# Two copies out of PSUM, a later place for the down projection's weight sums, and one PSUM tile moved from one pool to another

## The chip, the cores and the metric

The kernel runs on one core of a Trainium2 chip. The metric is the device time of one execution in microseconds (us); lower is better. The kernel before takes 2284.2 us (median of three runs, 2281.11 to 2285.95). The profile was taken from one more execution, whose own time is 2281.2 us; its span, from the first to the last recorded instruction, is 2279.5 us.

## The reference

The program computes a decoder trunk of two residual layers on 1024 tokens of width 1024. Each layer has a token mixer (layer 0: a gated MLP and dilated attention; layer 1: gated linear attention) and, behind it, a gated feed-forward network with a causal convolution. The change touches the feed-forward part and the end of the mixer's output projection before it:

```
x = x + mix
h = rms_norm(x, norm_ffn_g[layer])
g = causal_dwconv(h @ w_gate, conv_w, conv_b)        # width 3
x = x + (silu(g) * (h @ w_up)) @ w_down              # D_FF = 2816
```

All values are float32.

## The kernel before

**Products.** TensorE multiplies numbers of a reduced float32 format (F32R). To keep float32's accuracy every operand is split into a high part (ScalarE, "ACT", rounds it: the cast in line 92) and a low part (VectorE, "DVE", subtracts: line 93). A product then takes three passes: high by high, high by low, low by high. One 512x128 by 512x512 product is 12 matmuls of 128x512.

**Seven products for eight.** The feed-forward matrices are multiplied in 2x2 blocks by a scheme with seven block products (of the Strassen-Winograd kind): sums of blocks take the place of the eighth product. `ffn_up` walks over pairs of feature tiles, f = 0, 2, ..., 20, and has two streams for each, "g" (gate) and "u" (up). A stream takes products in the order 1, 5, 6, 2, 7, 4, 3, and product 1 of the next stream is opened before 4 and 3 of the current one. Its left operands are weight blocks, or the sums S1 to S4 of weight blocks (line 211, on GpSimd, "POOL", but for the first pair on DVE). Its right operands lie ready in SBUF: the normalised tokens in `hq`, and sums of them in the three tiles `T3`.

**Banks.** Products 1, 6, 7 and 4 add up in one PSUM bank, called B. Products 5 and 3 add up in bank C, product 2 has bank A. Between them the values are taken out: after 1 ACT copies B to `s1` (line 244), after 2 DVE adds `s1` and A to the block C11 (246), after 6 ACT copies B to C12 (248), after 7 ACT copies B to C22 (250) and DVE adds bank C, which then holds product 5 alone, to it (251); after 4 ACT copies B to C21 (253), after 3 DVE adds C, now products 5 and 3, to C12 (255). Matmuls of product 3 write to bank C, so they come behind the reading in line 251. The name `pgB6` is bank B of the gate stream of f = 6, and `wg6p7` is the left operand of its product 7. Banks B and C come from a pool `m1`, bank A and the transposes of the norm from a pool `pt`.

**After the streams.** Behind a pair's "g" stream follow the convolution (`conv`, lines 262 to 269: ACT scales, DVE adds two shifted terms, ACT applies silu) and `down_weights`, which loads two feature tiles of w_down (`rd`), forms four sums of their blocks on DVE (D, lines 280 to 283) and stores them to DRAM (`wsd`), for the down projection. Behind the "u" stream the two results are multiplied (line 324), and `down_acts` forms and stores sums of them (`actd`). The sums S and D and the temporaries of the norm share one ring of four SBUF tiles (tag "S"), and all loaded weights one ring of four (tag "raw").

**Ramp.** Before the streams `out_second` makes the second half of the output projection token tile by token tile (products `po`), normalises each tile (line 129 squares, 133 scales), transposes it on TensorE (line 143, two PSUM tiles `pt` for each token tile) and brings it into the operands (lines 420 to 440). The `pt` tiles are freed by DVE (line 420, tiles 0 to 3) or ACT (line 428, tiles 4 to 7).

**Order.** The code's order gives priorities; a scheduler at compile time fixes one order of instructions for each engine, and waits between engines are semaphores. An engine runs its list strictly in order.

Of the kernel before, what the change touches and what calls it, by code (L numbers as in the profile page):

```python
# [54 lines left out]
def trunk(ctx: ExitStack, tc: tile.TileContext, a, out):  # L55
    nc = tc.nc
    V, A, G, T, Q = nc.vector, nc.scalar, nc.gpsimd, nc.tensor, nc.sync
# [37 lines left out]
    def load_raw(src, name, cols=D):  # L95
        raw = rawp.tile([P, D], F32, tag="raw", name=name)[:, :cols]
        Q.dma_start(raw, src)
        return raw

    def parts_of(src, name, pool=None, **tag):  # L100

        w = (pool or wp).tile([P, 2, 512], F32R, **(tag or {"tag": "w"}), name=name)
        parts = [w[:, i, : src.shape[-1]] for i in range(2)]
        split(parts, src)
        return parts
# [86 lines left out]
    def ffn_up(l, T3, ps, pool, norm_end):  # L192
        cw = pool.tile([P, NF, 3], F32, name=f"cw{l}")
        Q.dma_start(cw, a["conv_w"][l])
        cb = pool.tile([P, NF], F32, name=f"cb{l}")
        Q.dma_start(cb, a["conv_b"][l])
        right = {1: hq[0][0], 2: hq[1][0], 3: hq[1][1], 4: hq[0][1], 5: T3[0], 6: T3[1], 7: T3[2]}

        def stream(kind, f):

            src = a["w_gate" if kind == "g" else "w_up"]
            ra, rb = (load_raw(src[l, f + i], f"r{kind}{f + i}") for i in range(2))
            A11, A12, A21, A22 = ra[:, :512], ra[:, 512:], rb[:, :512], rb[:, 512:]
            out = pool.tile([P, 2, S], F32, tag=kind, bufs=1, name=f"{kind}{f}")
            (C11, C12), (C21, C22) = ([out[:, i, c] for _, c in HALVES] for i in range(2))
            s1 = pool.tile([P, 512], F32, tag="s1", bufs=2, name=f"s1{kind}{f}")
            sums, bank, made = {}, {}, {}

            def summed(name, x, y, op):
                sums[name] = pool.tile([P, 512], F32, tag="S", bufs=4, name=f"{name}{kind}{f}")  # L210
                (G if f else V).tensor_tensor(sums[name], x, y, op=op)  # L211
                return sums[name]

            def left(p):
                if p == 5:
                    return summed("S1", A21, A22, ALU.add)
                if p == 6:
                    return summed("S2", sums["S1"], A11, ALU.subtract)
                if p == 7:
                    return summed("S3", A11, A21, ALU.subtract)  # L220
                if p == 3:
                    return summed("S4", A12, sums["S2"], ALU.subtract)
                return {1: A11, 2: A12, 4: A22}[p]

            def prep(p):
                made[p] = parts_of(left(p), f"w{kind}{f}p{p}")

            def step(p):
                if p not in made:
                    prep(p)  # L230
                L = made[p]

                b = {2: "A", 5: "C", 3: "C"}.get(p, "B")
                more = b in bank
                if not more:
                    bank[b] = ps.tile([P, 512], F32, tag="pt" if b == "A" else "m1", name=f"p{kind}{b}{f}")
                o = bank[b]
                for j in range(4):
                    for ii, jj in PASSES:
                        T.matmul(o, L[ii][:, j * P : j * P + P], right[p][:, jj, j, :], skip_group_check=more,  # L240
                                 start=(not more and j == 0 and (ii, jj) == PASSES[0]),
                                 stop=(j == 3 and (ii, jj) == PASSES[-1]))
                if p == 1:
                    A.copy(s1, o)
                elif p == 2:
                    V.tensor_add(C11, s1, o)
                elif p == 6:
                    A.copy(C12, o)
                elif p == 7:
                    A.copy(C22, o)  # L250
                    V.tensor_add(C22, C22, bank["C"])
                elif p == 4:
                    A.copy(C21, o)  # L253
                elif p == 3:
                    V.tensor_add(C12, C12, o)  # L255

            return step, out, prep

        def conv(f, g2):
            ts = []  # L260
            for i in range(2):
                g = g2[:, i, :]
                t = pool.tile([P, S], F32, tag="t", bufs=4, name=f"t{f + i}")
                w = lambda j: cw[:, f + i, j : j + 1]
                A.activation(t, g, AF.Identity, bias=cb[:, f + i : f + i + 1], scale=w(2))  # L265
                V.scalar_tensor_tensor(t[:, 1:], g[:, : S - 1], w(1), t[:, 1:], op0=ALU.mult, op1=ALU.add)  # L266
                V.scalar_tensor_tensor(t[:, 2:], g[:, : S - 2], w(0), t[:, 2:], op0=ALU.mult, op1=ALU.add)
                A.activation(t, t, AF.Silu)
                ts.append(t)
            return ts  # L270

        def put(dst, f, p, src):
            Q.dma_start(dst[l][p][f // 4][:, f // 2 % 2, :], src)

        def down_weights(f):

            ra, rb = (load_raw(a["w_down"][l, f + i], f"rd{f + i}") for i in range(2))
            A11, A21, A12, A22 = ra[:, :512], ra[:, 512:], rb[:, :512], rb[:, 512:]
            S = {p: pool.tile([P, 512], F32, tag="S", bufs=4, name=f"D{p}{f}") for p in (5, 6, 7, 3)}
            V.tensor_add(S[5], A21, A22)  # L280
            V.tensor_sub(S[6], S[5], A11)
            V.tensor_sub(S[7], A11, A21)
            V.tensor_sub(S[3], A12, S[6])
            for p in S:
                put(wsd, f, p, S[p])

        def down_acts(f, t0, t1):

            (B11, B12), (B21, B22) = ([t[:, c] for _, c in HALVES] for t in (t0, t1))
            x, y = (pool.tile([P, 2, 512], F32, tag="t", bufs=4, name=f"{n}{f}") for n in "xy")  # L290
            right = {1: B11, 2: B21, 3: B22, 5: x[:, 0], 6: x[:, 1], 7: y[:, 0], 4: y[:, 1]}
            V.tensor_sub(right[5], B12, B11)
            V.tensor_sub(right[6], B22, right[5])
            V.tensor_sub(right[7], B22, B12)
            V.tensor_sub(right[4], B21, right[6])
            for p in right:
                put(actd, f, p, right[p])

        todo = [(kind, f) for f in range(0, NF, 2) for kind in "gu"]
        cur, nxt = stream(*todo[0]), stream(*todo[1])  # L300
        for step, _, _ in (cur, nxt):
            step(1)
            step(2)
            if step is cur[0]:
                for prep, p in ((nxt[2], 1), (nxt[2], 2), (cur[2], 5)):
                    prep(p)
                norm_end()
        for i, (kind, f) in enumerate(todo):
            step, out, _ = cur
            early = (1, 2) if i < 2 else (1,)  # L310
            for p in (5, 6, 2, 7):
                if p not in early:
                    step(p)
            if 0 < i < len(todo) - 1:
                nxt = stream(*todo[i + 1])
                nxt[0](1)
            step(4)
            step(3)
            if kind == "g":
                ts = conv(f, out)  # L320
                down_weights(f)
            else:
                for j in range(2):
                    V.tensor_mul(ts[j], ts[j], out[:, j, :])  # L324
                down_acts(f, *ts)
            cur = nxt


# [572 lines left out]
    def banks(st, **bufs):  # L901
        return Tagged({t: st.enter_context(tc.tile_pool(name="psf_" + t, bufs=b, space=PSUM, reuse_waits="tile"))
                       for t, b in bufs.items()})
# [4 lines left out]
    ps = banks(pss, mm=3, pt=2)  # L908
    for l in range(2):
# [22 lines left out]
        with tc.tile_pool(name=f"T{l}", bufs=1, reuse_waits="tile") as tp:  # L932
            T3 = [tp.tile([P, 2, 4, 512], F32R, name=f"T{l}{i}") for i in range(3)]
            pss.close()
            with ExitStack() as st, tc.tile_pool(name=f"fu{l}", bufs=1, reuse_waits="tile") as fp:
                ps = banks(st, m1=6, pt=2)
                norm_end = out_second(l, w_out, x_in, T3, ps, fp)
                ffn_up(l, T3, ps, fp, norm_end)
        ps = banks(pss, mm=3, pt=2)
# [99 lines left out]
```

## Time and profile before

| what | before |
|---|---|
| median of three runs | 2284.2 us |
| profiled execution, its time / its span | 2281.2 us / 2279.5 us |
| PE (matmul) busy | 2193.6 us, 96% |
| DVE busy | 1443.9 us, 63% |
| ACT busy | 968.8 us, 43% |
| POOL busy | 453.3 us, 20% |
| share of PE in the chain of waits that ended last | 73% |

PE is busy for nearly the whole span, so the time is PE's work plus the moments in which it waits or runs at a lower granted clock. The feed-forward streams run from about 525 to 972 us in layer 0 and from about 1620 to 2065 us in layer 1. Times of single instructions are given in microseconds from the span's start.

### The profile page before, as it was taken

To read this page: it belongs to the slowest core of one execution; us is meant where nothing else is said; L and a number is where in the kernel's file an instruction comes from. 1 tells how busy PE (TensorE), PEld (TensorE's weight loads), DVE (VectorE), ACT (ScalarE), POOL (GpSimd) and SP (SyncE) were. 2 spreads that over 40 slices of the span, in tenths; PEclk is the share of its full clock that TensorE was granted. 3 is DMA by queue.
4 is the path that set the end of the run, shared out by engine and by line. 5 is a ranking of instruction groups with operands and counts; after the bars stand their busy time and mean duration, and the time that the engine had idled before them with its cause. 6 is when DMAs were issued, how large, how long until landed. Compare 5 with 4: busy or idle time off the path is not lost.

```text
span 2279.5 us, 29790 instructions
## 1 busy us (share of the span) xinstructions
PE 2193.6 (96%) x10800; PEld 1855.7 (81%) x10800; DVE 1443.9 (63%) x2430; ACT 968.8 (43%) x1786; POOL 453.3 (20%) x487
## 2 busy tenths in 40 slices
PE   7989988997999999999999999999899999999999
PEld 6989977886888888778889888878678887887887
DVE  7566655448777877755574444244787878776554
ACT  5444445235444343434454333223554444444443
POOL 4333220001242424100010111000133333230000
PEclk9999999998999999999999999999999999999999
DMA  4122212343354545475562111355254454457555
GB/s 145 47 73 78 60 50 61 124 145 106 130 171 141 178 137 168 157 282 185 202 224 75 54 54 51 121 180 184 71 171 162 148 170 149 141 178 263 199 190 203
DMA packets 139540, 320.74 MB, mean 141 GB/s; under 512 B 15824, under 2 KB 40400, under 8 KB 139392
## 3 DMA queue, kind: packets, MB, share of 16 engines
q1 hardware_dynamic: 139392, 318.83, 42.0%
q8 instruction: 85, 1.39, 0.2%
q14 instruction: 63, 0.52, 0.1%
HBM read 223.81 MB, written 94.96 MB: 140 GB/s over the span
## 4 chain that ended last, share of the span: by engine, by line
PE 73%; DVE 11%; DMA 6%; issue 5%; ACT 3%; POOL 2%; SPq 0%; DVEq 0%; POOLq 0%; ACTq 0%
PE puB L240 8%; PE pgB L240 7%; PE po L171 6%; PE pv L171 5%; PE pdB L345 5%; PE pdC L345 5%; PE pgC L240 5%; PE pj L171 4%; PE pdO L345 4%; PE pr L171 4%; PE puC L240 3%; PE puA L240 2%; PE pdQ L345 2%; PE pdP L345 2%; PE pk L183 2%
## 5 line engine op out<-in xcount | busy, mean ns | idle before, releaser
L93 DVE TENSOR_TENSOR da<-ar,da 128x512 fp32r<-128x512 f32 x154 | 106.3, 690 | 156.6 <-ACT da L92 156.3
L92 ACT CAST da<-ar 128x512 fp32r<-128x512 f32 x154 | 95.9, 623 | 214.8 <-PE pdC L345 94.7
L171 PE MATMUL po<-wo,hq 128*128 128x512 f32 x768 | 183.9, 394 | 2.2 <-ACT hq L395 1.3
L171 PEld LDWEIGHTS po<-wo,hq 128*128 128x128 f32 x768 | 141.9, 188 | 31.4 <-ACT hq L395 2.3
L171 PE MATMUL pj<-wq,hq 128*128 128x384 f32 x768 | 157.5, 353 | 1.5 <-ACT hq L92 1.5
L171 PE MATMUL pv<-wv,hq 128*128 128x256 f32 (+2 forms) x960 | 154.9, 314 | 0.7 <-ACT gv L507 0.6
L171 PEld LDWEIGHTS pv<-wv,hq 128*128 128x128 f32 x960 | 133.8, 191 | 9.3 <-ACT gv L507 1.0
L171 PEld LDWEIGHTS pj<-wq,hq 128*128 128x128 f32 x768 | 137.3, 197 | 2.2 <-ACT hq L92 1.9
L345 PE MATMUL pdB<-dw,da 128*128 128x512 f32 x528 | 136.4, 391 | 1.7 <-DVE u L255 1.6
L345 PE MATMUL pdC<-dw,da 128*128 128x512 f32 x528 | 135.8, 390 | 0.0
L345 PEld LDWEIGHTS pdB<-dw,da 128*128 128x128 f32 x528 | 98.5, 188 | 23.7 <-DVE u L255 2.4
L211 POOL TENSOR_TENSOR S1u<-ru 128x512 f32<-128x512 f32 x20 | 41.2, 2059 | 384.0 <-DMA wsd<-D 251.0
L93 DVE TENSOR_TENSOR dw<-wr,dw 128x512 fp32r<-128x512 f32 x154 | 105.8, 687 | 16.2 <-ACT dw L92 15.9
L345 PEld LDWEIGHTS pdC<-dw,da 128*128 128x128 f32 x528 | 99.1, 188 | 20.5
L121 POOL TENSOR_SCALAR rn<-ssq 128x1 f32<-128x1 f32 x32 | 8.5, 267 | 475.2 <-ACT h L129 257.3
L345 PE MATMUL pdO<-dw,da 128*128 128x512 f32 x396 | 102.2, 389 | 0.1
L92 ACT CAST dw<-wr 128x512 fp32r<-128x512 f32 x154 | 95.0, 617 | 13.6 <-DMA wr<-in_w_dn 7.7
L171 PE MATMUL pr<-wr,hq 128*128 128x512 f32 x384 | 97.9, 404 | 0.0
L345 PEld LDWEIGHTS pdO<-dw,da 128*128 128x128 f32 x396 | 74.3, 188 | 15.9 <-DVE dw L93 0.6
L171 PEld LDWEIGHTS pr<-wr,hq 128*128 128x128 f32 x384 | 71.2, 188 | 14.5
L324 DVE TENSOR_TENSOR t<-t,u 128x1024 f32<-128x1024 f32 x44 | 75.6, 1717 | 5.4 <-ACT u L253 4.8
L266 DVE SCALAR_TENSOR_TENSOR t<-g,cw,t 128x1023 f32<-128x1023 f32 x44 | 56.5, 1324 | 6.9 <-ACT t L265 6.8
(905 smaller groups left out, 5106.4 us busy)
## 6 DMA issues: line engine op xcount, KB each, us to landing
ar<-actd SPq DMA_DIRECT2D x70, 512.0 KB, 3.6
rg<-in_w_gate SPq DMA_DIRECT2D x44, 512.0 KB, 5.1
ru<-in_w_up SPq DMA_DIRECT2D x44, 512.0 KB, 3.6
rd<-in_w_down SPq DMA_DIRECT2D x44, 512.0 KB, 3.6
wsd<-D SPq DMA_DIRECT2D x88, 256.0 KB, 2.3
wr<-wsd SPq DMA_DIRECT2D x40, 512.0 KB, 4.3
actd<-t SPq DMA_DIRECT2D x66, 256.0 KB, 5.5
wr<-in_w_dn SPq DMA_DIRECT2D x30, 512.0 KB, 4.7
```

Of the source, the lines that this page charges most:

```text
L92: (hi or A.copy)(dst[0], src)
L93: (lo or V.tensor_sub)(dst[1], src, f32(dst[0]))
L121: G.tensor_scalar(r, ssq, 1.0 / n, EPS, op0=ALU.mult, op1=ALU.add)
L171: T.matmul(o, L[i], R[jj][:, sl], start=(k == 0 and (ii, jj) == PASSES[0]), stop=(k == nk - 1 and (ii, jj) == PASSES[-1]))
L183: T.matmul(ps[h], L[i], hq[k % 2][h][:, jj, k // 2, :], start=(k == 0 and (ii, jj) == PASSES[0]), stop=(k == KD - 1 and (ii, jj) == PASSES ...
L211: (G if f else V).tensor_tensor(sums[name], x, y, op=op)
L240: T.matmul(o, L[ii][:, j * P : j * P + P], right[p][:, jj, j, :], skip_group_check=more, start=(not more and j == 0 and (ii, jj) == PASSES ...
L266: V.scalar_tensor_tensor(t[:, 1:], g[:, : S - 1], w(1), t[:, 1:], op0=ALU.mult, op1=ALU.add)
L324: V.tensor_mul(ts[j], ts[j], out[:, j, :])
L345: T.matmul(o, L[ii][:, t * P : t * P + P], R[jj], skip_group_check=more, start=start and not more and (ii, jj) == PASSES[0], stop=stop and ...
```

## The change

Three edits. Product 5 has an evacuation of its own: right behind it ACT copies bank C to C22. Behind product 7 ACT copies bank B to `s1` (free again by then) and DVE adds `s1` to C22, both from SBUF. The call of `down_weights` moves from the end of the pair's "g" stream to the end of its "u" stream, behind `down_acts`. And in the two pools of PSUM that `out_second` and `ffn_up` use, `m1` has 5 tiles in place of 6, `pt` has 3 in place of 2.

```
                 elif p == 6:
                     A.copy(C12, o)
+                elif p == 5:
+                    A.copy(C22, o)
                 elif p == 7:
-                    A.copy(C22, o)
-                    V.tensor_add(C22, C22, bank["C"])
+                    A.copy(s1, o)
+                    V.tensor_add(C22, C22, s1)
...
             if kind == "g":
                 ts = conv(f, out)
-                down_weights(f)
             else:
                 for j in range(2):
                     V.tensor_mul(ts[j], ts[j], out[:, j, :])
                 down_acts(f, *ts)
+                down_weights(f)
...
-                ps = banks(st, m1=6, pt=2)
+                ps = banks(st, m1=5, pt=3)
```

Lines behind the edit move by two: the copies and adds of the list above are lines 250 to 257 in the changed kernel. The scheduler makes another order of all that lies in the ramps and the streams; the rest of the program stands as before. Three places follow.

TensorE in the middle of the streams (f = 6, layer 0), the kernel before:

```order
L240 MATMUL pgB6_6560<-T02_5153,wg6p7_6678 128x512 x12
L240 MATMUL puB6_6704<-hq00_83,wu6p1_6701 128x512 x12
L240 MATMUL puC6_6783<-T00_5151,wu6p5_6780 128x512 x10
L240 MATMUL pgB6_6560<-hq01_84,wg6p4_6718 128x512 x12
L240 MATMUL pgC6_6628<-hq11_86,wg6p3_6736 128x512 x12
L240 MATMUL puC6_6783<-T00_5151,wu6p5_6780 128x512 x2
L240 MATMUL puB6_6704<-T01_5152,wu6p6_6798 128x512 x12
```

The same place in the changed kernel:

```order
L240 MATMUL pgB6_6550<-T02_5153,wg6p7_6685 128x512 x12
L240 MATMUL puB6_6711<-hq00_83,wu6p1_6708 128x512 x2
L240 MATMUL pgC6_6634<-hq11_86,wg6p3_6743 128x512 x12
L240 MATMUL puC6_6774<-T00_5151,wu6p5_6771 128x512 x8
L240 MATMUL pgB6_6550<-hq01_84,wg6p4_6725 128x512 x12
L240 MATMUL puC6_6774<-T00_5151,wu6p5_6771 128x512 x4
L240 MATMUL puB6_6711<-T01_5152,wu6p6_6790 128x512 x12
```

Product 3 (`pgC6`, operand `wg6p3`) stands two matmuls behind product 7 now and ahead of product 4; before, it stood 34 matmuls behind product 7, after product 4.

ACT at the same place, from the end of pair 6's gate stream on, in the kernel before:

```order
L250 COPY g6_6555<-pgB6_6560 128x512
L92 CAST wg8p1_6856<-rg8_6850 128x512
L244 COPY s1u6_6700<-puB6_6704 128x512
L92 CAST wu6p4_6873<-ru7_6697 128x512
L253 COPY g6_6555<-pgB6_6560 128x512
L92 CAST wu6p3_6891<-S4u6_6889 128x512
L92 CAST wg8p5_6924<-S1g8_6922 128x512
L92 CAST wg8p6_6942<-S2g8_6940 128x512
L265 ACTIVATE t6_6752<-g6_6555,cb0_5665,cw0_5663 128x1024
L265 ACTIVATE t7_6757<-g6_6555,cb0_5665,cw0_5663 128x1024
L248 COPY u6_6699<-puB6_6704 128x512
```

And in the changed kernel:

```order
L252 COPY s1g6_6546<-pgB6_6550 128x512
L92 CAST wg8p1_6848<-rg8_6842 128x512
L244 COPY s1u6_6707<-puB6_6711 128x512
L92 CAST wu6p4_6865<-ru7_6704 128x512
L92 CAST wu6p3_6883<-S4u6_6881 128x512
L267 ACTIVATE t6_6759<-g6_6545,cb0_5665,cw0_5663 128x1024
L255 COPY g6_6545<-pgB6_6550 128x512
L267 ACTIVATE t7_6764<-g6_6545,cb0_5665,cw0_5663 128x1024
L250 COPY u6_6706<-puC6_6774 128x512
L270 ACTIVATE t6_6759<-t6_6759 128x1024
L92 CAST wg8p5_6932<-S1g8_6930 128x512
L248 COPY u6_6706<-puB6_6711 128x512
```

The copy of product 5 (line 250) is new, and the copy of bank B to C12 of the u stream (line 248) stands right behind the cast of `S1g8`, a sum that now takes its SBUF tile from the stored sums D of pair 6.

DVE where the streams begin (layer 0, f = 0), the kernel before:

```order
L93 TENSOR_TENSOR wg0p3_5856<-S4g0_5854,wg0p3_5856 128x512
L280 TENSOR_TENSOR D50_5886<-rd0_5882,rd1_5884 128x512
L281 TENSOR_TENSOR D60_5887<-D50_5886,rd0_5882 128x512
L282 TENSOR_TENSOR D70_5888<-rd0_5882 128x512
L283 TENSOR_TENSOR D30_5889<-rd1_5884,D60_5887 128x512
L211 TENSOR_TENSOR S1u0_5898<-ru1_5675 128x512
```

And in the changed kernel:

```order
L211 TENSOR_TENSOR S4g0_5855<-rg0_5667,S2g0_5802 128x512
L211 TENSOR_TENSOR S1u0_5883<-ru1_5675 128x512
L93 TENSOR_TENSOR wg0p6_5804<-S2g0_5802,wg0p6_5804 128x512
L93 TENSOR_TENSOR wg0p7_5822<-S3g0_5820,wg0p7_5822 128x512
L93 TENSOR_TENSOR wg0p4_5839<-rg1_5669,wg0p4_5839 128x512
L93 TENSOR_TENSOR wg0p3_5857<-S4g0_5855,wg0p3_5857 128x512
L211 TENSOR_TENSOR S2u0_5902<-S1u0_5883,ru0_5673 128x512
```

The first sum of the up stream, `S1u0`, stands ahead of the first sum D of w_down now (that one comes ten rows behind the last row shown); before, it stood behind all four.

## Rows read from the trace of the kernel before

**Rows 1.** The page, busy us and share of the span by engine.

```profile
PE 2193.6 (96%) x10800; PEld 1855.7 (81%) x10800; DVE 1443.9 (63%) x2430; ACT 968.8 (43%) x1786; POOL 453.3 (20%) x487
```

**Rows 2.** Windows over both feed-forward parts: ramp (two), streams, end; each layer.

```profile
core 0: us, PE busy (x) PEld busy (x) DVE busy (x) ACT busy (x) POOL busy (x), PEclk, DMA share, GB/s
518.00:546.00 28.00, 22.95 (x105) 17.92 (x104) 25.52 (x43) 20.27 (x45) 3.39 (x4) 0.88 0.13 43
546.00:570.00 24.00, 17.27 (x60) 12.66 (x59) 17.70 (x29) 8.58 (x16) 3.72 (x3) 0.86 0.58 175
570.00:957.00 387.00, 383.14 (x1686) 315.95 (x1685) 299.12 (x339) 166.83 (x261) 131.15 (x78) 1.00 0.48 157
957.00:975.00 18.00, 15.64 (x67) 11.98 (x66) 14.40 (x18) 9.25 (x13) 0.00 (x0) 1.00 0.40 117
1612.00:1640.00 28.00, 23.00 (x102) 18.20 (x102) 24.68 (x41) 19.29 (x44) 3.39 (x4) 0.88 0.08 29
1640.00:1658.00 18.00, 14.18 (x52) 10.26 (x52) 13.73 (x23) 5.94 (x11) 0.00 (x0) 0.91 0.42 134
1658.00:2050.00 392.00, 385.86 (x1697) 317.93 (x1696) 305.41 (x346) 167.94 (x266) 135.67 (x80) 1.00 0.49 159
2050.00:2068.00 18.00, 15.68 (x66) 11.97 (x65) 14.59 (x18) 9.25 (x13) 0.00 (x0) 1.00 0.38 120
```

**Rows 3.** PE's waits by releaser, 505 to 990 and 1590 to 2085: total, times, longest.

```profile
PE pgC L240 <- DVE g L251: 3.9, 4, 1.0
PE puC L240 <- ACT wu0p L92: 3.6, 1, 3.6
...
PE pgC L240 <- DVE g L251: 6.1, 5, 2.1
```

**Rows 4.** Chain that ended last, layer 0, 640 to 720: start, us, what.

```profile
660.96 3.61 DMA rd<-in_w_down
...
665.41 2.03 DMA wsd<-D
...
667.66 2.07 POOL S1u L211
...
679.59 1.70 DVE y L294
...
681.95 3.02 PE pgC L240 x12
...
685.42 2.72 PE puB L240 x12
```

**Rows 5.** Timeline of ACT, layer 0: start, us, line, instruction, idle before.

```profile
579.23 1.28 ACT L268 ACT_TABLE_LOAD   x1
...
659.02 0.59 ACT L250 COPY u<-puB 128x512 f32<-128x512 f32 x1 [1.66 <-PE puB L240]
...
669.75 0.62 ACT L92 CAST wu6p<-S1u 128x512 fp32r<-128x512 f32 x1 [2.44 <-POOL S1u L211]
...
686.09 2.38 ACT L265 ACTIVATE t<-g,cb,cw 128x1024 f32<-128x1024 f32 x2
```

**Rows 6.** Line 251 on DVE: ns min/median/max, first and last start.

```profile
L251 DVE TENSOR_TENSOR g<-g,pgC x22: 672/674/681, 562.5 to 2042.2; 128x512 f32<-128x512 f32 x22
```

**Rows 7.** Chain that ended last, ramp of layer 0.

```profile
561.31 1.22 PE puC L240 x2
562.53 5.10 PE pgB L240 x12
```

**Rows 8.** Timeline of DVE, ramp of layer 0.

```profile
506.53 0.75 DVE L133 TENSOR_SCALAR xt<-xt,rn 128x1024 f32<-128x1024 f32 x1 [2.55 <-DMA xd<-xt]
...
516.80 0.75 DVE L133 TENSOR_SCALAR xt<-xt,rn 128x1024 f32<-128x1024 f32 x1 [2.35 <-ACT n L428]
```

**Rows 9.** Timeline of PE, end of the streams of layer 0.

```profile
965.83 3.02 PE L240 MATMUL puB<-hq,wu20p 128*128 128x512 f32 x12 [1.31 <-ACT u L250]
...
972.35 1.66 PE L345 MATMUL pdB<-dw,da 128*128 128x512 f32 x6 [0.78 <-DVE u L255]
```

More of the change, by code (lines that the diff above doesn't have):

```diff
@@ L248, in step @@
                     A.copy(C12, o)
+                elif p == 5:
+                    A.copy(C22, o)
                 elif p == 7:
-                    A.copy(C22, o)
-                    V.tensor_add(C22, C22, bank["C"])
+                    A.copy(s1, o)
+                    V.tensor_add(C22, C22, s1)
                 elif p == 4:
@@ L320, in ffn_up @@
                 ts = conv(f, out)
-                down_weights(f)
             else:
@@ L325, in ffn_up @@
                 down_acts(f, *ts)
+                down_weights(f)
             cur = nxt
@@ L935, in trunk @@
             with ExitStack() as st, tc.tile_pool(name=f"fu{l}", bufs=1, reuse_waits="tile") as fp:
-                ps = banks(st, m1=6, pt=2)
+                ps = banks(st, m1=5, pt=3)
                 norm_end = out_second(l, w_out, x_in, T3, ps, fp)
```

## Prediction

> **What bounds the kernel now.** I read the page's busy line first: PE is busy for 96% of the span, DVE for 63%, ACT for 43%, POOL for 20% [rows 1]. PE works 2193.6 of 2279.5 us, so no edit that leaves its matmuls alone can give more than some 86 us. The number of matmuls stays. What can be won is PE's idle time in the stretches whose order changes, and matmuls that ran there at a lower clock. The windows give the ceiling [rows 2]: window less PE busy is 5.05 and 6.73 us in the two parts of layer 0's ramp, 3.86 in its streams, 2.36 at their end; in layer 1 it is 5.00, 3.82, 6.14 and 2.32. That is 20.6 us in ramps, 10.0 in streams, 4.7 at the ends. The clock is full in streams and at the ends (PEclk 1.00) and 0.86 to 0.91 in the ramps.
>
> The waits then say what the idle time is. In the streams there is one kind: product 3's first matmul waits for DVE's line 251, 3.9 us in four waits in layer 0 and 6.1 in five in layer 1 [rows 3], which is all of the 3.86 and 6.14. The chain through such a place shows why DVE is late [rows 4]: a load `rd` of w_down (3.61 us) starts at 660.96, a store `wsd` of a sum D (2.03) at 665.41, POOL's sum S1u, whose SBUF tile that store frees, at 667.66, and later a 1.70 us subtraction on DVE, behind which line 251 comes; `pgC` follows at 681.95. Line 251 itself is short (0.67 us) [rows 6]; it stands in DVE's in-order list behind work that waited for weights.
>
> **The change part by part: streams.** The bank C of a "g" stream is now freed by ACT's copy right behind product 5; by the order product 3 follows 48 matmuls later (10.9 us), and nothing of DVE stands between. The 10.0 us go unless something else is late next. What is late next I count backward and forward in PE's slots. A product is 12 matmuls of 2.72 us together [rows 4], 0.227 each. I take the end of the g stream's product 3 as zero. Product 7 ends two matmuls and product 3 earlier, at −3.2. ACT then has a copy (0.59 [rows 5]), a cast, a copy and a cast (0.62 each cast), to −0.8; DVE takes the low half of that operand (about 0.7, as any of its 128x512 work in rows 6), to −0.1. That frees the weight tile into which `rd` is loaded. Its load 3.61: at 3.5. First sum D 0.7: 4.2. Store 2.03 [rows 4]: 6.3. POOL's S1 of the next gate stream 2.07: 8.4. ACT's cast of it: 9.0. Behind this cast stands the copy of B to C12 in the u stream (line 248), 0.59: 9.6. Product 7 of u, which writes to that bank, has its slot at 13.4: between zero and it stand u's 5, 6 and 2, g's 4 and eleven matmuls of the next gate's 1, 59 x 0.227. So the new wait of ACT has 3.8 us of cover. Product 5 of the next gate stream is due 25 matmuls later, 19.0, and has its operand at about 10.7: 8 us of cover. The copy after product 7 must be done before product 4, 5 us later. Five tiles of `m1` are enough: a bank B lives some 12 slots, a bank C some 7, and at most four are live at a time.
>
> The 44 extra copies (22 pairs, two streams each) are 44 x 0.59 = 26 us of ACT, which is idle for half of the streams (166.8 of 387 us busy [rows 2]). Their price lies between 0 and 26; I take 0, as that idle time and the slots above cover it. The add into C22 reads only SBUF now. Its nearest rows are 0.67 with PSUM [rows 6] and 1.70, the SBUF-only subtraction in rows 4: 0 to 44 x 1.03 = 45 us of DVE. I take 0 for PE, because after the change no matmul waits for this add before the convolution's or u's product, over 5 us on.
>
> By a rule of the Trainium skill ("SBUF — State Buffer", section "Who interferes with whom") a DVE instruction with two SBUF inputs shares a port with GpSimd and one shuts the other out, while with at most one SBUF input it does not. By that rule each add into C22 could become a 1.70; the trace agrees in that line 251 never exceeds 0.68 [rows 6]. The same rule is rival D's.
>
> **Ramps.** In layer 0 PE waits 3.6 us for `wu0p`, the operand made of S1u0 [rows 3], and 14 matmuls after it take 1.22 + 5.10 = 6.32 us in place of 14 x 0.227 = 3.17 [rows 7]: the clock had fallen after the idle time. S1u0 stood behind four sums D, thus behind a load of w_down; now it stands before them. The wait and the slow matmuls go: 3.6 + 3.1 = 6.7 us. Layer 1 has no such wait in rows 3, so nothing there.
>
> DVE is what paces the transposes before that (25.5 of 28 us busy [rows 2]). It has two gaps, 2.55 us for a residual tile and 2.35 for ACT's line 428 [rows 8], both through the two `pt` tiles and the order; a third tile lets later transposes run ahead. Bounds: 0 and 4.9 us in a layer; I take 4.0, nearer the upper end, since with more transposes done DVE has work for both gaps. Of it 0.6 is paid back because S1u0 now precedes a low half which PE needs: 3.4 in a layer, and the same for layer 1, whose idle time in this part is equal (5.00 against 5.05). Both: 6.8.
>
> A cost stands against it. In the first pair, where the pipeline isn't filled yet, ACT's copy to C12 of u0 stands behind a cast that waits for the first stores of D and for POOL, and behind a table load of 1.28 [rows 5]. My schedule from above, shifted for the shorter distance, makes product 7 of u0 about 1.1 us late, 2.2 in both layers. Bounds: 0 to 3.3 in a layer (the late cast's 2.07 of POOL and a copy more).
>
> **Ends.** The last streams idle 1.31 us for the copy after product 7 and 0.78 for DVE's last add [rows 9]. The copy remains, since product 4 of u20 follows its 7 directly; the second and 0.26 of small gaps go, as DVE has less to do there: about 1.05 in a layer, 2.1 in both. Bounds 0 to 4.7, the windows' idle time.
>
> **Sum.** 10.0 + 6.7 + 6.8 + 2.1 − 2.2 = 23.4 us less. The profiled execution took 2281.2 (span 2279.5 and 1.7 around it) and would take 2257.8. It lies 3.0 under the median of 2284.2 and within the runs' spread, so against the median: 2260.8. Its own range, with the ramps' bounds (down 1.8 and the ends' 2.6 more; up 6.8 and 4.4), is about 2255 to 2268.
>
> **Rivals.**
>
> B, the ramp stays paced by DVE. For it: 25.5 of 28 us busy. Then the 6.8 go and a gap of S1u0's place is paid, 1.2: 15.4 gained, 2268.8.
>
> C, streams: the wait is not removed but moves to another product (u's 5 or 7, the next gate's 5), because the load and store chain of rows 4 is as long as before and only its place changes. Against it: 3.8 and 8 us of cover. Gain 13.4: 2270.8.
>
> A, the other side: ACT's list is in order, and line 248 of each u stream hangs behind the cast of the next S1, so behind load, D, store and POOL. Place: before product 7 of u. Each us beyond the 3.8 of cover is paid in some 20 pairs. It decides from 3.8 + 23.4/20 = 5.0 us of delay against my schedule. DMA is busy for half of the streams [rows 2] and the load waits for a tile and a place in a queue, so a chain 6 us later than I count is possible: 2.2 x 20 = 44 lost against 23.4 gained, 2304.8. Against it: the 8.8 us of rows 4 (from the load's start to POOL's end) hold such delays already.
>
> D, the add into C22 takes 1.70 while POOL reads SBUF, DVE gets 45 us longer, and it reaches PE: 2260.8 + 45 = 2305.8. For it: a 1.70 row exists. Against it: DVE is idle for 88 of 387 us in streams, and POOL has a pause when the gate stream's add is due. The rule of the Trainium skill cited above would give this time if nothing covered it.
>
> E, the copies and the ramp's new wait eat the rest, or the pools' order makes other small waits: about 2284, the change does nothing that can be told.
>
> **How the numbers follow.** Forecast 0.52, B 0.19, C 0.11, E 0.07, A 0.08, D 0.03. A measurement tells about 0.2%, 4.6 us, from no change. Faster: 0.52 + 0.19 + 0.11 = 0.82; same: E, 0.07; slower: A and D, 0.11. The range takes in the forecast, B and C with some 3 us more, 2250 to 2274, and leaves out E, A and D, 0.18; its low end is the sum with the ramps' and ends' bounds (4.4 us), the 2.2 of the ACT wait not paid, and the 3 us that the profiled run is under the median.
>
> **What would show it.** Right: no wait of `pgC` on line 253 and no idle time in the streams' windows; no wait for `wu0p`, and a clock near 1.00 behind it; less idle time of DVE among line 133's rows; a wait of 1 us at u0's product 7 alone. Wrong: PE waits for line 248 in the middle pairs (A), waits for other operands (C), adds of line 253 of 1.7 with a matmul behind them (D), a ramp of the same length (B).

## The result and the profile after

The changed kernel takes 2251.9 us (median of four runs, 2247.3 to 2255.6) against 2284.1 before: ratio 0.9859, 95% interval 0.9838 to 0.9880, 32.2 us less. Forecast were 23.4 us less and 2260.8 us. The profiled execution has a span of 2249.7 us, 29.8 less than before.

The page's busy line of the changed kernel, in the order of [rows 1]:

```profile
PE 2184.3 (97%) x10800; PEld 1853.6 (82%) x10800; DVE 1487.9 (66%) x2430; ACT 988.7 (44%) x1830; POOL 476.9 (21%) x487
```

PE is busy for 9 us less with the same 10800 matmuls (fewer of them ran at the lower clock or behind a wait), and idle for 20.5 us less. ACT's 44 added copies show as 20 us, DVE has 44 us more.

The windows answer to [rows 2], same columns; because layer 1 starts 12 us earlier now, its windows are earlier too:

```profile
516.00:544.00 28.00, 24.49 (x109) 19.22 (x107) 25.08 (x41) 18.00 (x41) 3.03 (x4) 0.94 0.06 20
544.00:568.00 24.00, 21.49 (x82) 17.22 (x83) 19.42 (x28) 13.36 (x21) 4.58 (x4) 0.86 0.51 168
568.00:941.00 373.00, 373.00 (x1647) 308.86 (x1646) 321.31 (x338) 171.16 (x275) 139.48 (x77) 1.00 0.49 163
941.00:956.00 15.00, 14.32 (x63) 11.56 (x62) 10.04 (x13) 8.04 (x13) 0.00 (x0) 1.00 0.35 119
1600.00:1628.00 28.00, 23.36 (x110) 17.88 (x108) 26.55 (x44) 18.91 (x43) 3.02 (x4) 1.00 0.05 19
1628.00:1646.00 18.00, 16.49 (x73) 13.61 (x73) 16.01 (x23) 9.75 (x16) 1.36 (x1) 1.00 0.53 166
1646.00:2021.00 375.00, 375.00 (x1656) 310.49 (x1656) 320.89 (x340) 172.71 (x279) 147.01 (x79) 1.00 0.49 165
2021.00:2035.50 14.50, 13.82 (x61) 11.14 (x60) 10.05 (x13) 7.75 (x12) 0.00 (x0) 1.00 0.37 122
```

In both layers the streams have no idle PE time (373.00 of 373.00, 375.00 of 375.00) where before they had 3.86 and 6.14. The ends are down to 0.68 each, and the ramps still have 6.0 and 6.2 us. PE's waits in layer 0's feed-forward part (releaser, us in total, times, longest) are now those of the ramp and one copy at the end, and neither `wu0p` nor line 251's successor is in the list [rows 3]:

```profile
PE pgB L240 <- ACT hq L92: 2.3, 1, 2.3
PE pgC L240 <- ACT wg0p L92: 1.5, 1, 1.5
PE pgB L240 <- ACT wg0p L92: 1.5, 1, 1.5
...
PE puB L240 <- ACT s1u L252: 0.7, 1, 0.7
```

I measure the feed-forward part in PE's timeline from its first matmul of the output projection behind the mixer's last transposes to the first matmul of the down projection. Before, it took 507.4 us in layer 0 and 506.5 in layer 1; after, 493.0 and 489.0. So 14.4 + 17.5 = 31.9 us came from the places that the prediction names, and the rest of the program is 2.1 us longer in this execution, with the same order. The ramp I measure from the same start to the end of the 168th matmul of line 240 (14 products). It took 118.3 and 114.9 us before and takes 111.2 and 107.2 after: 14.8 us less. Of the 17.1 that remain, 4.3 are the ends and 12.8 the streams.

### The profile page after: what moved, and what is told of

Read it like the earlier page. It is cut to its first block, busy times and chain, and to the rows that moved or that the text cites. A ratio compares the mean times of both kernels' runs of the same rounds, so it can differ in the third digit from the quotient of the medians.

```text
span 2249.7 us, 29889 instructions
## 1 busy us (share of the span) xinstructions
PE 2184.3 (97%) x10800; PEld 1853.6 (82%) x10800; DVE 1487.9 (66%) x2430; ACT 988.7 (44%) x1830; POOL 476.9 (21%) x487
## 4 chain that ended last, share of the span: by engine, by line
PE 86%; DVE 5%; DMA 3%; ACT 3%; issue 3%; POOL 1%; SPq 0%; ACTq 0%; DVEq 0%; POOLq 0%
PE pgB L240 11%; PE puB L240 11%; PE po L171 6%; PE puC L240 5%; PE pgC L240 5%; PE pv L171 5%; PE pdB L347 5%; PE pdC L347 5%; PE pj L171 5%; PE pdO L347 4%; PE pr L171 4%; PE pgA L240 3%; PE puA L240 2%; PE pdQ L347 2%; PE pdP L347 2%
## 5 line engine op out<-in xcount | busy, mean ns | idle before, releaser
L347 PEld LDWEIGHTS pdC<-dw,da 128*128 128x128 f32 x528 | 99.1, 188 | 20.5
L211 POOL TENSOR_TENSOR S1g<-rg 128x512 f32<-128x512 f32 x20 | 27.6, 1381 | 409.0 <-DMA wsd<-D 285.5
L269 DVE SCALAR_TENSOR_TENSOR t<-g,cw,t 128x1022 f32<-128x1022 f32 x44 | 75.9, 1724 | 0.1
```

The lines of the kernel that those rows point to most:

```text
L347: T.matmul(o, L[ii][:, t * P : t * P + P], R[jj], skip_group_check=more, start=start and not more and (ii, jj) == PASSES[0], stop=stop and ...
```

## The experiments

Each kernel was timed beside the kernel before on the same chip, in 4 to 12 executions (the kernel before takes 2282.3, 2283.1 and 2283.8 us in the three groups).

| kernel | copies | move | pools | us | less than before | ratio, 95% interval |
|---|---|---|---|---|---|---|
| copies | yes | | | 2273.2 | 9.1 | 0.994 to 0.997 |
| place | | yes | | 2260.1 | 22.2 | 0.988 to 0.991 |
| pools | | | yes | 2271.3 | 11.0 | 0.994 to 0.997 |
| copies_place | yes | yes | | 2257.3 | 25.0 | 0.987 to 0.990 |
| copies_pools | yes | | yes | 2260.2 | 23.6 | 0.989 to 0.992 |
| place_pools | | yes | yes | 2252.2 | 30.9 | 0.985 to 0.988 |
| whole | yes | yes | yes | 2254.4 | 28.7 | 0.986 to 0.990 |
| presum | | (sums S ahead of D) | | 2258.0 | 25.1 | 0.988 to 0.991 |
| place0 | | first pair only | | 2278.9 | 4.9 | 0.997 to 0.999 |
| placeN | | all but the first | | 2270.0 | 13.8 | 0.993 to 0.995 |
| g0 | yes | yes | yes, S on POOL | 2251.4 | 31.7 | 0.985 to 0.988 |
| pp_g0 | | yes | yes, S on POOL | 2258.1 | 25.8 | 0.988 to 0.991 |

**The copies alone.**

```
+                elif p == 5:
+                    A.copy(C22, o)
                 elif p == 7:
-                    A.copy(C22, o)
-                    V.tensor_add(C22, C22, bank["C"])
+                    A.copy(s1, o)
+                    V.tensor_add(C22, C22, s1)
```

> Only the two copies out of PSUM (product 5 by ACT; product 7 by ACT into s1, DVE's add from SBUF); the sums of w_down stay behind the gate stream and the pools stay 6 and 2. My theory: the waits of product 3 in the streams (10.0 us, and about 0.2 us more for each of the nine waits because PE's pipeline is empty after one) and part of the idle time at the streams' ends go with this edit alone: 13 to 17 us less, about 2269, no wait of pgC on DVE in the streams, and the 3.6 us wait for wu0p in layer 0's ramp remains. Rival: the waits come from the sums of w_down that stand ahead in DVE's list, so that the edit only moves them to another product: under 5 us less.

9.1 us less, between the theory's 13 and the rival's 5. The nine waits for line 251 are gone, as expected. The ramps are 4.6 and 2.3 us shorter, which neither had: the wait for `wu0p` did not stay at 3.6 us but fell to 1.9. But one new wait came in each layer, in pair 2 (2.97 and 3.62 us), and takes back most of what the nine had cost: behind the ramps only 4.9 us are gained. The timelines of PE, ACT and DVE in layer 0 (start, us, engine, instruction, idle time before it and what ended it):

```profile
600.39 4.54 PE L240 MATMUL pgB<-hq,wg2p 128*128 128x512 f32 x12 [2.97 <-ACT s1g L252]
```

```profile
599.75 0.59 ACT L252 COPY s1g<-pgB 128x512 f32<-128x512 f32 x1 [6.82 <-DVE g L246]
```

```profile
592.76 2.31 DVE L326 TENSOR_TENSOR t<-t,u 128x1024 f32<-128x1024 f32 x1
...
596.68 1.76 DVE L295 TENSOR_TENSOR x<-t,x 128x512 f32<-128x512 f32 x1
...
598.97 0.67 DVE L246 TENSOR_TENSOR g<-s1g,pgA 128x512 f32<-128x512 f32 x1
```

The copy of product 7 goes into `s1`, and `s1` must first be read by DVE's line 246. That one stands in DVE's list behind operations of 1.8 to 2.3 us. ACT waits for it 6.8 us, PE 2.97, and the twelve matmuls behind it take 4.34 us until the next row in place of 2.72. With the copies PE no longer waits for DVE through bank C, but in one pair of each layer through `s1`; there the rival was right, not for the other pairs.

**The move alone.**

```
                 ts = conv(f, out)
-                down_weights(f)
...
                 down_acts(f, *ts)
+                down_weights(f)
```

> Only the move of the sums of w_down behind the up stream. My theory: the 3.6 us wait for wu0p in layer 0's ramp and the slow matmuls behind it go (6.7 us); the waits of product 3 on DVE's line 251 stay, for bank C is still freed by DVE: 5 to 8 us less, about 2277.5. Rival: the sums of w_down in DVE's list were the whole cause of the late line 251, so the waits in the streams go too: 15 us or more less. Another: the load of w_down, now one stream later, makes operands late in each pair: slower than before.

22.2 us less: the rival. The waits for `wu0p` and all the waits of product 3 are gone, though DVE still frees bank C. At the place that answers to [rows 4], POOL, DVE and PE show why:

```profile
649.37 1.67 POOL L211 TENSOR_TENSOR S1u<-ru 128x512 f32<-128x512 f32 x1 [2.96 <-DVE wg6p L93]
...
658.08 1.61 POOL L211 TENSOR_TENSOR S4u<-ru,S2u 128x512 f32<-128x512 f32 x1 [1.29 <-DVE wg6p L93]
```

```profile
667.61 0.68 DVE L251 TENSOR_TENSOR g<-g,pgC 128x512 f32<-128x512 f32 x1
...
675.14 0.69 DVE L280 TENSOR_TENSOR D<-rd,rd 128x512 f32<-128x512 f32 x1 [3.79 <-DMA rd<-in_w_down]
```

```profile
674.30 2.88 PE L240 MATMUL pgC<-hq,wg6p 128*128 128x512 f32 x12
```

POOL has made the four sums of `u6` by 659.7; before, it started them at 667.66, released by the store of a D [rows 4]. So line 251 is done at 668.3, and product 3 comes at 674.30: 6 us to spare, where before it was 1 us late. The D sums, and the wait for their load, come behind line 251.

**The pools alone.**

```
-                ps = banks(st, m1=6, pt=2)
+                ps = banks(st, m1=5, pt=3)
```

> Only the pools (m1 5, pt 3). My theory: the transposes of tokens 4 and 5 run earlier, so that the idle time of PE before product 1 (4.6 us of waits for pt on DVE in layer 0, 4.4 in layer 1) shrinks by 2 to 3 us in each layer, and in layer 1 the clock stays at its upper level, worth 5 us more: 6 to 11 us less, about 2275; the waits in the streams and for wu0p stay. Rival: DVE paces the ramp and the third tile gives nothing: within 2 us of before. Rival: five tiles of m1 are too few where product 7 is evacuated by two readers, and the streams wait more: slower.

11.0 us less, and the waits for line 251 stay (3.7 and 6.9 us); the wait for `wu0p` shrinks to 2.1. The ramps are 5.4 and 4.7 us shorter (112.9 and 110.2): PE's waits for the transposes (4.6 and 4.4) have become one wait for ACT's cast of `hq` (2.1 and 1.9). What five tiles of `m1` cost can't be told from one profile: behind the ramps layer 0 is 2.0 us shorter than before, layer 1 2.9 longer.

**Copies and move, without the pools**: the first two diffs together.

> Both copies and the move, the pools as before (6 and 2): the whole change without its pools. My theory: the sum of the two parts, 20 to 24 us less, about 2262; the ramp's waits for pt and, in layer 1, the low clock stay; against the whole change this is 8 to 11 us slower. Rival: the parts overlap (the move alone or the copies alone would have removed the same waits): no faster than the better of the two.

25.0 us less, 2.8 more than the move alone, with intervals that overlap. What the copies took away alone they do not take away a second time.

**The whole change again**, on the chip of the next three kernels.

> The changed kernel itself, as the measure for the runs beside it: about 2252, with 32 us less than before in the two feed-forward parts, no wait of product 3 on DVE in the streams.

28.7 us less. This run's profile, one of its slower executions (2260.1), holds the wait that the prediction placed at product 7 of `u0`. PE, ACT and POOL there:

```profile
573.36 4.23 PE L240 MATMUL puB<-T,wu0p 128*128 128x512 f32 x12 [2.15 <-ACT u L248]
```

```profile
569.84 0.62 ACT L92 CAST wg2p<-S1g 128x512 fp32r<-128x512 f32 x1 [5.46 <-POOL S1g L211]
...
572.74 0.57 ACT L248 COPY u<-puB 128x512 f32<-128x512 f32 x1
```

```profile
567.38 2.43 POOL L211 TENSOR_TENSOR S1g<-rg 128x512 f32<-128x512 f32 x1 [33.70 <-DMA wsd<-D]
```

The chain is the predicted one: the store of a D, POOL's S1 of the next gate stream, its cast, the table load, and behind them line 248. It cost 2.15 us, and the twelve matmuls behind it took 1.3 us more than 2.72. The first profile has no such wait. Counted from the ramp's start, PE was ready for product 7 at 102.7 us here and at 105.3 there, where slow matmuls had held it up, and line 248 began at 104.2 here and 103.0 there, where POOL's S1 had taken 1.35 us.

**Move and pools, without the copies**: the second and third diff.

> The move and the pools without the two copies. The move alone has taken the waits of product 3 away already (22 us less than before), so my first theory, by which the copies do it, is in doubt. Theory now: the waits come from where D stands, the copies are needed only where D stands early, so without them the whole change's time is kept but for the streams' ends: 2252 to 2256. Rival (my first theory): bank C, still freed by DVE, is late again once the ramp is shorter or m1 has five tiles: 5 to 12 us slower than the whole change.

30.9 us less, not slower than the whole change (28.7 on the same chip; the intervals overlap). The waits of product 3 do not come back. The copies are worth nothing that these runs can tell once the sums D have moved.

**The sums S ahead of the sums D**, which stay in their place behind the gate stream.

```
                 ts = conv(f, out)
+                for p in (5, 6, 7, 3):
+                    nxt[2](p)
                 down_weights(f)
```

> The kernel before with one edit: the four sums S of the up stream are asked for ahead of down_weights, so that they take their SBUF tiles before D does; D stays in its place in DVE's list, ahead of line 251, and bank C is freed by DVE as before. Theory: the waits in the streams come from POOL's S1u, which waits for the store of a sum D before it, and so puts all of POOL's eight sums beside DVE's busiest stretch: with S ahead, the waits of product 3 (10 us) and the 3.6 us wait for wu0p go, about 15 us less. Rival: they come from D's own work in DVE's list, which waits for the load of w_down there: the waits stay, under 5 us less, and only the wait for wu0p goes.

25.1 us less: the theory, and more. The two feed-forward parts are as short as with the move alone (495.5 and 493.4 us, against 495.5 and 493.7). POOL and DVE at f = 6:

```profile
644.37 1.74 POOL L211 TENSOR_TENSOR S1u<-ru 128x512 f32<-128x512 f32 x1
...
656.99 1.28 POOL L211 TENSOR_TENSOR S4u<-ru,S2u 128x512 f32<-128x512 f32 x1 [1.61 <-DVE wg6p L93]
```

```profile
660.08 0.69 DVE L280 TENSOR_TENSOR D<-rd,rd 128x512 f32<-128x512 f32 x1
...
670.20 0.68 DVE L251 TENSOR_TENSOR g<-g,pgC 128x512 f32<-128x512 f32 x1
```

The first sum D still stands ahead of line 251 in DVE's list, and bank C is still freed by line 251, but the S sums no longer wait for a store. Line 251 is early, and product 3 waits nowhere. So the cause of the waits was the order in the shared ring of four SBUF tiles: with D asked for first, S1u got its tile only when the first D was stored.

How a late S1u makes line 251 late is in the trace of the kernel before. Released by that store, POOL makes seven sums from 667.66 to 680.75 with hardly a pause, and they run beside DVE's products and subtractions. POOL and DVE there:

```profile
672.76 1.74 POOL L211 TENSOR_TENSOR S4u<-ru,S2u 128x512 f32<-128x512 f32 x1
...
679.07 1.68 POOL L211 TENSOR_TENSOR S3g<-rg,rg 128x512 f32<-128x512 f32 x1 [0.63 <-DVE wu6p L93]
```

```profile
673.27 2.32 DVE L324 TENSOR_TENSOR t<-t,u 128x1024 f32<-128x1024 f32 x1
...
679.51 1.78 DVE L294 TENSOR_TENSOR y<-t,t 128x512 f32<-128x512 f32 x1
```

The same two in the kernel with S ahead, where POOL stands still at that time:

```profile
666.06 1.22 DVE L326 TENSOR_TENSOR t<-t,u 128x1024 f32<-128x1024 f32 x1
...
669.60 0.69 DVE L294 TENSOR_TENSOR y<-t,t 128x512 f32<-128x512 f32 x1
```

Of the 40 products of line 324 in the streams of the kernel before, the 20 that start while a POOL instruction runs take 2.30 to 2.32 us, the other 20 1.21 to 1.23, also where POOL starts during them. Between S1u's cast and line 251 at f = 6, six of DVE's instructions are longer in this way, by 4.8 us together. From the low half of S4g to line 251 DVE needs 19.7 us before and 13.4 with S ahead: 4.8 of these 6.3 us are the six instructions, the rest is shorter waiting. One thing is not held apart: with S ahead DVE hardly waits for the load of w_down either (2.8 us ahead of layer 0's first sums D, 16.1 before), so what that wait alone would do is not shown.

**The move for the first pair alone, and for all the others.**

```
+                if f:            # place0; placeN: if not f:
                     down_weights(f)
...
                 down_acts(f, *ts)
+                if not f:        # placeN: if f:
+                    down_weights(f)
```

> The kernel before with one edit: down_weights moves behind the up stream for the first pair only; the other ten pairs of each layer are as before. It sizes the ramps' part of the move. Theory: S1u0 before the sums D is worth 6 to 7 us in layer 0 (3.6 us of waiting and the slow matmuls behind it) and, against my prediction, 5 to 6 us in layer 1 too, where no wait names it: there the up stream's operands were late all the same, and PE's order put three products of the gate stream in a row, each waiting for a copy; 10 to 13 us less in all, and product 3's waits in the streams remain. Rival (the prediction's step): nothing in layer 1, 6 to 7 us less in all.

> The opposite: down_weights moves for all pairs but the first. It sizes the streams' part. Theory: the waits of product 3 go (10.0 us and 0.2 us more for each of nine), the ramps stay as before: 10 to 13 us less, and with place0 it adds up to the whole move, 22. Rival: the gain of the move needs the first pair, because lateness there is handed from pair to pair: under 5 us less.

13.8 for the others, as expected. 4.9 for the first pair, under both expectations. Its profile is of the longest of its twelve executions (2284.4). In it the ramps are 6.5 and 1.9 us shorter, but the streams of layer 0 gave part of it back, in waits for line 251 (8.3 us in place of 3.9):

```profile
PE pgC L240 <- DVE g L251: 8.3, 5, 3.5
```

The two parts sum to 18.7, against 22.2 for both at once. In placeN layer 1's ramp is 3.0 us longer than before (117.9 against 114.9), and the wait for `wu0p` stands in layer 1 too, where the kernel before has none:

```profile
PE puC L240 <- ACT wu0p L92: 3.6, 1, 3.6
```

So layer 1 has the same lateness in it; whether PE shows it as that wait depends on the order of its products.

**Copies and pools, without the move**: the first and third diff.

> The two copies and the pools, without the move: the one pair of edits not yet measured. Theory: the copies take the streams' waits away (about 12 us) and the pools 4 to 7 us in the ramps, but the copy behind product 7 of the first pair waits in ACT's list behind the late cast of S1u0 (3.0 and 3.6 us where the copies stand alone), so the sum is 14 to 20 us less: slower than the whole change by 10 us or more, for the move is the part that can't be spared. Rival (my first theory): the copies are the main part, and the time is within 7 us of the whole change.

23.6 us less, more than the theory had; by gains, each against its own before, it is 5.1 behind the whole change beside its neighbours (28.7) and 8.6 behind the first measurement (32.2), so the rival's 7 holds only against the former. The rival's reason does not hold, for place_pools has the whole change's time without the copies. Copies and move are substitutes, not parts of a sum. The wait for line 252 that the copies alone have is still there, 1.5 us in layer 0 and 3.6 in layer 1; in the copies' own trace it comes from line 246 on DVE, not from the cast of S1u0 that the theory named.

**The sums S of the first pair on POOL**, in the whole change and in the one without copies.

```
-                (G if f else V).tensor_tensor(sums[name], x, y, op=op)
+                G.tensor_tensor(sums[name], x, y, op=op)
```

> The changed kernel, with the sums S of the first pair on POOL like all the others, not on DVE. Theory: DVE paces what is left of the ramps (6 us of PE's idle time in each layer); its eight sums of 0.69 us are 5.5 us less for it in each ramp, while POOL is idle there: 2 to 6 us less than the whole change in both layers together. Rival: POOL takes 1.3 to 2.3 us for each, S2 needs S1, and PE waits for these operands now (1.5 us twice in each ramp): the waits grow by 1 to 3 us in each layer and the time is longer.

> The move and the pools, without the copies, and the sums of the first pair on POOL: the two versions that were as fast as the whole change or a little faster, put together. Theory: as the copies are not needed once D has moved, 2249 to 2253, no slower than the whole change. Rival: without the copies bank C is late in the first pair where POOL's sums come later than DVE's: 2255 or more.

g0 is 3.0 us below the whole change on the same chip, with intervals that overlap: no difference that can be told. pp_g0 is no gain either (25.8); PE waits for the operands that POOL now makes, in layer 0 2.6 us for `wg0p` and 2.5 for `wu0p`.

None of the other kernels is clearly faster than the changed kernel; place_pools has its time with one edit less.

## Why the prediction was right, and which step was not

**Time and sign** were right, with little to spare: 2251.9 lies 1.9 us above the lower end of 2250 to 2274, and the gain is 8.8 us larger than forecast. (The forecast's own range is added up wrongly: its bounds give 2256.4 to 2272.0, not 2255 to 2268. The measured time lies below either; it is inside the stated range through the 2.2 us of a wait not paid and the 3 us of the profiled run.) 31.9 us came out of the two feed-forward parts, 23.4 were forecast. By terms: streams 10.0 forecast, 12.8 measured; ends 2.1 and 4.3; ramps 11.3 (6.7 + 6.8 − 2.2) and 14.8.

**Streams: the wait went, but the step that says why was incomplete.** The prediction let the 10.0 us go because ACT frees bank C, and gave the move no share in it. It had DVE late "behind work that waited for weights"; the larger part, where the trace was taken apart, is that POOL's bunched sums make DVE's own instructions longer (4.8 of 6.3 us at f = 6). That the copies suffice is shown (no wait for line 251 in the kernel with them alone), but so does the move alone, and so does asking for S ahead of D. The chain of [rows 4] that the prediction quoted (store of D, POOL's S1u, late DVE) was the cause; the move takes it apart at its root, and with it the copies have nothing left to do. That the term came out although the move was left out of it is luck: either edit removes the wait, and it was counted once. Rival C was wrong for the whole change, yet right for the copies alone in one pair of each layer: there the wait moved to `s1`.

The schedule behind "3.8 us of cover" can be held against the trace. ACT, DVE and POOL in the changed kernel at f = 6, and PE:

```profile
672.87 0.69 DVE L282 TENSOR_TENSOR D<-rd,rd 128x512 f32<-128x512 f32 x1
```

```profile
675.81 1.30 POOL L211 TENSOR_TENSOR S1g<-rg 128x512 f32<-128x512 f32 x1 [19.75 <-DMA wsd<-D]
```

```profile
677.17 0.60 ACT L92 CAST wg8p<-S1g 128x512 fp32r<-128x512 f32 x1
677.68 0.58 ACT L248 COPY u<-puB 128x512 f32<-128x512 f32 x1
```

```profile
666.52 2.88 PE L240 MATMUL pgC<-hq,wg6p 128*128 128x512 f32 x12
669.24 1.98 PE L240 MATMUL puC<-T,wu6p 128*128 128x512 f32 x8
...
682.61 2.88 PE L240 MATMUL puB<-T,wu6p 128*128 128x512 f32 x12
```

Zero, the end of product 3, is 666.52 + 2.88 = 669.40. The first D was forecast at 3.5 and stands at 3.5; POOL's S1 at 6.3 and 6.4; its cast from 8.4 and 7.8 (POOL took 1.30 us, not 2.07); line 248 done at 9.6 and 8.9; product 7 of u at 13.4 and 13.2. Rival A had 4 us of distance in the steady pairs, and bit only in the first pair, in one of two profiles.

**Size of the streams' term.** The prediction took the idle time that the waits show. Three rows of PE in the kernel before, around one such wait:

```profile
678.09 2.88 PE L240 MATMUL pgB<-hq,wg6p 128*128 128x512 f32 x12
681.95 3.02 PE L240 MATMUL pgC<-hq,wg6p 128*128 128x512 f32 x12 [0.97 <-DVE g L251]
684.80 0.61 PE L240 MATMUL puC<-T,wu6p 128*128 128x512 f32 x2
```

The product before it starts at 678.09 and is 2.72 us of work, so PE could have gone on at 680.81; it went on at 681.95, 1.14 later, of which 0.97 are shown as idle. The twelve matmuls behind it took 2.85 in place of 2.72. This wait costs 0.30 us more than its row says; if all nine do, that is 2.7 us, the difference between 10.0 and 12.8. The ends had three waits in each layer and now have one, which is 1.2 us more for both, and about half of the copy's wait went too (1.31 before, 0.68 after), which the prediction had kept.

**Ramps.** In layer 0, 9.0 us were forecast and 7.1 measured (5.8 in the second profile): the wait for `wu0p` went, but in the first profile not the slow matmuls; they stand behind two waits for `wg0p`. PE in the changed kernel's ramp, first profile:

```profile
545.00 0.73 PE L240 MATMUL pgB<-T,wg0p 128*128 128x512 f32 x2 [1.45 <-ACT wg0p L92]
547.25 1.22 PE L240 MATMUL pgC<-hq,wg0p 128*128 128x512 f32 x2 [1.51 <-ACT wg0p L92]
548.26 4.47 PE L240 MATMUL pgB<-T,wg0p 128*128 128x512 f32 x10
```

The last row's ten matmuls take 4.27 us until the next row, in place of 2.27 (granted clock 0.62 from 545 to 554). In the second profile the same ten, behind the same two waits, take 2.28:

```profile
553.35 2.44 PE L240 MATMUL pgB<-T,wg0p 128*128 128x512 f32 x10
```

In layer 1, 2.3 were forecast and 7.7 measured, and here the clock gave what it took in layer 0. Two rows of PE in the kernel before, layer 1, and the first of them in the kernel with the move alone:

```profile
1625.80 4.20 PE L240 MATMUL pgB<-hq,wg0p 128*128 128x512 f32 x11
...
1645.88 4.14 PE L240 MATMUL pgB<-T,wg0p 128*128 128x512 f32 x10 [1.02 <-DVE wg0p L93]
```

```profile
1619.04 2.86 PE L240 MATMUL pgB<-hq,wg0p 128*128 128x512 f32 x11
```

Until the next instruction or wait they took 4.03 and 4.15 us before (granted clock 0.67 and 0.72 in the 6 us around), 2.63 and 2.28 in the changed kernel: 3.3 of the 7.7 us, for which the prediction had no term. Of the other 4.4, 2.3 were forecast and 1.1 is the wait at line 248 that did not come here. What is left, about 1 us by these numbers, is the step that failed: "Layer 1 has no such wait in rows 3, so nothing there". The lateness of S1u0 was there, and PE's order hid its name: in placeN, with this order of D and S1u0 kept, it shows as 3.6 us. The 4.2 us by which the move alone shortens layer 1's ramp (114.9 to 110.7) do not size it, for 3.1 of them are the same two rows at the higher clock (2.69 and 2.40 us), behind waits as long. The pools' term held: 6.8 forecast, 6.0 measured between place (112.5 and 110.7) and place_pools (108.7 and 108.5); the pools alone shortened the ramps by 10.1. The wait at line 248, 1.1 us a layer, came in one profile of two, with 2.15 us in one layer.

**Rival D.** The add into C22 from SBUF, all 44 (ns: min, median, max):

```profile
L253 DVE TENSOR_TENSOR g<-g,s1g x22: 679/695/1783, 564.0 to 2013.2; 128x512 f32<-128x512 f32 x22
L253 DVE TENSOR_TENSOR u<-u,s1u x22: 678/679/1775, 573.8 to 2032.7; 128x512 f32<-128x512 f32 x22
```

Two of the 44 reach 1.8 us, and in both a POOL instruction was running when the add began, as the rule of the Trainium skill ("SBUF — State Buffer", section "Who interferes with whom") lets one expect for a DVE instruction with two SBUF inputs beside POOL; line 251 with its PSUM input never passed 0.69 (0.681 in "g" [rows 6], 0.689 in "u"). But the median is 0.68 to 0.70: for 24 adds POOL stands still, for 18 its next instruction starts only after the add has begun, and these adds stay at 0.68. No matmul waits for the add.

**What stays open**: how the 3.5 us by which the whole change's two measurements differ (32.2 and 28.7 less) divide between chips and the first pair's wait; and why place0 and placeN fall 3.5 us short of the whole move: the 3.0 us of placeN's ramp and the waits that place0 got in its streams point to it, but each is read from one profile. How much of the ramps' gain is the granted clock varies from one execution to the next.

## What to carry to other kernels

When an engine is late behind its in-order list, follow the wait back past the engine to the buffer: here a sum waited for a tile that another kind of data had to leave by a store, and asking for the tiles in another order did more than a private copy for the late reader. Before adding up edits that act on one wait, ask of each whether it alone would remove the wait, for then they are substitutes. Where two engines share work, look also at whether one makes the other's instructions longer: here DVE's products took 2.3 us in place of 1.2 when they started beside POOL. Price a wait by the distance between the starts of the instructions around it, not by the idle time shown, and look for the same lateness where the order gives it another name.

## What the runs showed that was not expected

The granted clock behind the same waits is not the same from one execution to the next. Two kernels, place and place0, have the same order in layer 1's ramp from product 2 of u0 on, each with waits of 1.5 and 1.0 us ahead of these ten matmuls:

```profile
1637.58 2.57 PE L240 MATMUL pgB<-T,wg0p 128*128 128x512 f32 x10 [1.02 <-DVE wg0p L93]
```

```profile
1650.65 4.64 PE L240 MATMUL pgB<-T,wg0p 128*128 128x512 f32 x10 [1.02 <-DVE wg0p L93]
```

In the second the granted clock of the 20 us around was 0.83, in the first 1.00. Such stretches are worth 2 us each, and they move the ramps' time between executions of one kernel by as much as a small edit does.
